# The two ends of a trunk kernel: first weight tile in two transfers, closing root on ScalarE, output in one transfer per column half

## The chip, the cores and the metric

The kernel runs on one core of a Trainium2 chip. The metric is device time in microseconds (us) of one execution, as the median of several runs. Engines are named as the profile names them: PE (TensorE, matmuls) with its weight load PEld, DVE (VectorE), ACT (ScalarE), POOL (GpSimd) and SP (SyncE, which here only issues transfers). Transfers (DMAs) run on 16 DMA engines that the core has.

## The reference

A decoder trunk of two layers on x of 256 tokens by 2048 features, in float32. Each layer adds to x a token mixer (layer 0: chunked gMLP; layer 1: a complex-diagonal S5 state-space layer with a GLU), an attention to 256 memory rows and a squared-ReLU MLP with 8192 hidden features, each on a normalized input. The end is one more normalization. What the change touches of it is the first product and the last line:

```python
def rms_norm(x, g):
    xf = x.astype(F32)
    y = xf * lax.rsqrt(jnp.mean(xf * xf, axis=-1, keepdims=True) + EPS)
    return (y * g.astype(F32)).astype(x.dtype)

def chunked_gmlp(h, w_in, b_in, ln_g, ln_b, w_s, b_s, w_out):
    z = jax.nn.gelu(h @ w_in + b_in, approximate=False)
    u, v = jnp.split(z, 2, axis=-1)
    ...

def reference(x, mem, ...):
    for i in range(DEPTH):
        h = rms_norm(x, g_mix[i])
        x = x + chunked_gmlp(...) if i % 2 == 0 else x + s5_glu(...)
        x = x + memory_attention(...)
        x = x + squared_relu_mlp(rms_norm(x, g_ff[i]), f_w_up[i], f_w_down[i])
    return rms_norm(x, g_final)
```

## The kernel before

**Precision.** A float32 product is made of three float32r products: each operand is split into a high part (a cast on ACT, line 102) and a low part (source less high part, on DVE, line 103), and PE sums high x high, low x high and high x low. So every weight tile goes through three stages: a transfer into `wraw` (line 123), the two splits into `whi` and `wlo`, and the matmuls.

**Tiles.** The weights lie in memory as tiles of 128 partitions by 1024 floats (512 KB): two blocks of 128 input features by 512 output features. `Trunk.wload` issues the transfer of one tile on SP and remembers it as `self.fed`; `Trunk.wtile` loads (or takes a tile that was loaded ahead from the list `raw`) and splits. There are four `wraw` buffers (a fifth in some stages) and three each of `whi` and `wlo`. The order on every engine is the order of the code, moved by a scheduler: it respects the buffers, and `tc.issue_after(self.fed)` puts a transfer behind the weight load named.

**The start.** `gmlp` reads x transposed (`x_t`) in four chunks of four feature blocks; each chunk comes in two transfers of two blocks (128x512, 256 KB; lines 314 to 318, tile `memc`). `scale_chunk` (lines 242 to 249) multiplies each block by the norm's weight and splits it into `act`, on ACT (line 247) and DVE (line 248). Between the two transfers of the first chunk the first weight tile is loaded ahead (`first.append(...)`, line 320). `opening` then works on two column blocks of `a_w_in` in turn, numbers NCH and NCH + 1 (NCH is 4), tile by tile: the first tile of the one, the first of the other, the second of the one, and so on; the matmuls are at line 152. A tile has two feature blocks, so the first tile of either column block needs only the first transfer of x's first chunk.

**The end.** The last matrix product is `gemm_last`: its weights are split once and kept, and it runs over all 16 feature blocks first for token block t = 0 (128 tokens), then for t = 1 (PE lines 829 to 831). After each block it calls `FinalNorm.finish`. There, `gather` (DVE line 658) adds the product to x, 256 columns at a time; ACT squares and sums these (line 1414); DVE adds the two sums to the mean square of the other columns (line 1416), forms an approximate inverse root with an integer trick on the float's bits (line 1417) and refines it in three Newton steps (lines 1421 and 1422, `rstd_t` and `rstd`). x is then multiplied by the root (and, for the last 512 columns, by the norm's weight) in four pieces of 512 columns, two on DVE (lines 1423 and 1425) and two on ACT (lines 1424 and 1427). So block t = 0's closing runs while PE works on t = 1.

**The output.** The tokens lie permuted in x: partition 32q + c of block t is token 8c + 4t + q. A column half of a block is therefore written in four transfers, one for each q: 32 partitions by 1024 columns (128 KB), to every eighth row of the output (line 1430). They are issued on SP:

```python
self.out = out.rearrange("(c h q) d -> h q c d", h=2, q=4)
...
for cs in (slice(0, D // 2), slice(D // 2, D)):
    for q in range(4):
        nc.sync.dma_start(out=self.out[t, q][:, cs], in_=x[32 * q:32 * q + 32, t, cs])
```

**Two other transfers** that the prediction reads are in the S5 layer, the loads of `lb` at line 1054 on SP. Each fills 128 partitions by 512 floats, and its source has a pattern of 8 (T), 16 and 512 elements, the outermost first:

```python
src = (bass.AP(tensor=b.tensor, offset=b.offset, ap=[[0, T], [8 * 64, 16], [1, 8 * 64]]),
       bass.AP(tensor=Ld.tensor, offset=Ld.offset + q * 8 * 64, ap=[[G * 2 * 64, T], [0, 16], [1, 8 * 64]]))
with self.tc.issue_after(self.fed):
    nc.sync.dma_start(out=e["lb", q][:, i], in_=src[i])
```

Of the kernel before, what the change touches and what calls it, by code (L numbers as in the profile page):

```python
# [9 lines left out]
F32 = mybir.dt.float32  # L10
F32R = mybir.dt.float32r
I32 = mybir.dt.int32
AF = mybir.ActivationFunctionType
ALU = mybir.AluOpType
AX = mybir.AxisListType

P = 128
D = 2048
S = 256
KT = D // P  # L20
NB = 512
NCH = D // NB
KB = 2
# [15 lines left out]
class Trunk:  # L39
# [7 lines left out]
    def __init__(self, ctx, tc, a):  # L47
        self.ctx, self.tc, self.nc, self.a = ctx, tc, tc.nc, a
        nc = self.nc
        ent = ctx.enter_context  # L50
        self.const = ent(tc.tile_pool(name="const", bufs=1))
        self.main = ent(tc.tile_pool(name="main", bufs=1))
        self.act = ent(tc.tile_pool(name="act", bufs=2))
        self.wp = ent(tc.tile_pool(name="wp", bufs=3))
        self.sm = ent(tc.tile_pool(name="sm", bufs=2))
        self.dram = ent(tc.tile_pool(name="dram", bufs=1, space=bass.MemoryType.DRAM))
        self.psA = ent(tc.tile_pool(name="psA", bufs=2, space=bass.MemoryType.PSUM))
        self.psM = [ent(tc.tile_pool(name=f"psM{i}", bufs=2, space=bass.MemoryType.PSUM)) for i in range(2)]

        warm = self.const.tile([P, 1], F32, name="warm")  # L60
        nc.vector.memset(warm, 0.0)
        nc.scalar.activation(out=warm, in_=warm, func=AF.Gelu)
        self.ident = self.const.tile([P, P], F32, name="ident")
        make_identity(nc, self.ident)
        self.gcol = self.const.tile([P, 8, KT], F32, name="gcol")
        nc.scalar.dma_start(out=self.gcol, in_=a["gcol"])
        self.rstd_mem = None
        self.loads, self.fifth = 0, None
        self.side = []
        self.lag, self.every, self.now, self.plan = 100, 1, 0, []  # L70
# [42 lines left out]
        return t  # L113


    def wload(self, w, n, kc):
        self.loads += 1
        if self.fifth and self.loads % 5 == 0:
            raw = self.fifth.tile([P, KB * NB], F32, name="wraw", bufs=1)
        else:  # L120
            raw = self.wp.tile([P, KB * NB], F32, name="wraw", bufs=4)
        k, c = w.shape[3:]
        self.fed = self.nc.sync.dma_start(out=raw.rearrange("p (k c) -> p k c", k=k), in_=w[n, kc]).ins
        return raw

    def wtile(self, w, n, kc, raw=None):
        nc = self.nc
        raw = raw.pop() if raw else self.wload(w, n, kc)
        hi = self.wp.tile([P, KB * NB], F32R, name="whi")
        lo = self.wp.tile([P, KB * NB], F32R, name="wlo")  # L130
        self.low = self.split(hi, lo, raw)
        return [t.rearrange("p (k c) -> p k c", k=w.shape[3]) for t in (hi, lo)]

    def gemm_tok(self, act, w, n, acc=None, k0=0, kts=range(KT), first=True, last=True, raw=None):
# [171 lines left out]
    def gmlp(self, x, nxt):  # L306
        nc, a, tc = self.nc, self.a, self.tc
        with tc.tile_pool(name="gm", bufs=2, reuse_waits="tile") as gp:
            hT = self.new_act()
            ss = self.new_ss()  # L310
# [3 lines left out]
            def fetch(j):  # L314
                xt = xts[j] = gp.tile([P, 4, S], F32, name="memc", tag="u", bufs=5)
                for h in range(0, 4, 2):
                    with tc.issue_after(self.fed) if j else nullcontext():
                        nc.sync.dma_start(out=xt[:, h:h + 2], in_=a["x_t"][j][:, h:h + 2])
                    if j == 0 and h == 0:
                        first.append(self.wload(a["a_w_in"], NCH, 0))  # L320

            def features(j):
                self.scale_chunk(xts.pop(j), 0, hT, j)
# [6 lines left out]

            first = []
            fetch(0)
            features(0)
            rstd = None
# [18 lines left out]
            def opening(n0, outs):  # L353

                accs, bs = [None, None], []
                for k in range(NCH):
                    self.at((6, 8, 9, 11)[k], lambda k=k: tokens(k))
                for i in range(2):
                    self.at(10 + i, lambda i=i: bs.append(bias(n0 + i)))

                def step(i, kc):
                    accs[i] = self.gemm_tok(hT, a["a_w_in"], n0 + i, acc=accs[i], kts=range(KB * kc, KB * kc + KB),
                                            first=kc == 0, last=kc == KT // KB - 1, raw=first)

                order = [(i, kc) for kc in range(KT // KB - 2) for i in range(2)]
                order += [(i, KT // KB - 2 + kc) for i in range(2) for kc in range(2)]
                for m, (i, kc) in enumerate(order):
                    if m % 4 == 3 and m // 4 + 1 < NCH:
                        fetch(m // 4 + 1)
                    if m % 4 == 0 and 0 < m < 4 * NCH:  # L370
                        features(m // 4)
                    if m == len(order) - 2:
                        activate(n0, outs[0], accs[0], bs[0])
                    step(i, kc)
                activate(n0 + 1, outs[1], accs[1], bs[1])
# [23 lines left out]
            v = self.act.tile([P, 2, NCH, NB], F32, name="v", tag="act")  # L399
# [973 lines left out]
class FinalNorm:  # L1373
# [4 lines left out]

    def __init__(self, tr, out):
        self.tr = tr  # L1380
        self.out = out.rearrange("(c h q) d -> h q c d", h=2, q=4)

    def start(self):
        tr = self.tr
# [16 lines left out]
    def finish(self, x, t, gather):  # L1401

        tr, nc = self.tr, self.tr.nc
        v = nc.vector
        e = (NCH - 1) * NB
        pre, y, a = (tr.sm.tile([P, 1], F32, name=nm) for nm in ("rs_v", "rstd", "rstd_t1"))
        ss = self.end[:, t]
        v.tensor_reduce(out=pre, in_=self.ss[:, t:t + 1, 0:NCH - 1], axis=AX.X, op=ALU.add)
        v.tensor_scalar(out=pre, in0=pre, scalar1=1.0 / D, scalar2=EPS, op0=ALU.mult, op1=ALU.add)
        for h in range(2):  # L1410
            cs = slice(e + h * NB // 2, e + (h + 1) * NB // 2)
            gather(cs)
            junk = tr.sm.tile([P, NB], F32, name="junk", bufs=1)
            nc.scalar.activation(out=junk[:, 0:NB // 2], in_=x[:, t, cs], func=AF.Square, accum_out=ss[:, h:h + 1])
        for h in range(2):
            v.scalar_tensor_tensor(out=pre, in0=ss[:, h:h + 1], scalar=1.0 / D, in1=pre, op0=ALU.mult, op1=ALU.add)
        v.tensor_scalar(out=y.bitcast(I32), in0=pre.bitcast(I32), scalar1=-0.5,
                        scalar2=1597463007.0, op0=ALU.mult, op1=ALU.add)
        v.tensor_scalar(out=pre, in0=pre, scalar1=-0.5, scalar2=None, op0=ALU.mult)
        for _ in range(3):  # L1420
            v.scalar_tensor_tensor(out=a, in0=y, scalar=pre, in1=y, op0=ALU.mult, op1=ALU.mult)
            v.scalar_tensor_tensor(out=y, in0=a, scalar=1.5, in1=y, op0=ALU.add, op1=ALU.mult)
        v.tensor_scalar(out=x[:, t, 0:NB], in0=x[:, t, 0:NB], scalar1=y, scalar2=None, op0=ALU.mult)
        nc.scalar.activation(out=x[:, t, NB:2 * NB], in_=x[:, t, NB:2 * NB], func=AF.Copy, scale=y)
        v.scalar_tensor_tensor(out=x[:, t, e:], in0=x[:, t, e:], scalar=y, in1=self.g[NCH - 1],
                               op0=ALU.mult, op1=ALU.mult)
        nc.scalar.activation(out=x[:, t, 2 * NB:e], in_=x[:, t, 2 * NB:e], func=AF.Copy, scale=y)
        for cs in (slice(0, D // 2), slice(D // 2, D)):
            for q in range(4):
                nc.sync.dma_start(out=self.out[t, q][:, cs], in_=x[32 * q:32 * q + 32, t, cs])  # L1430


def regroup(tr, x):
# [101 lines left out]
```

## Time and profile before

| | |
|---|---|
| runs | 2793.18, 2794.51, 2795.72 us; median 2794.51 |
| profiled execution | 2790.06 us, of which the span is 2788.4 |
| mean granted clock of PE | 0.999 |
| PE busy | 2765.7 us, 99% of the span |
| DVE, ACT, POOL busy | 71%, 50%, 8% |
| DMA | 593.76 MB, mean 213 GB/s |

The span runs from the first recorded instruction to the end of the last. Busy times are shares of it. Where a row has an "xN", it groups N instructions; the number in front is the time from the first one's start to the last one's end in a timeline, and the sum of their durations in the lists of groups. A DMA share is the mean busy share of the 16 DMA engines in a stretch.

### The profile page before, as it was taken

How to read it: one execution, taken by the hardware profiler on the slowest of the kernel's cores; microseconds unless marked ns; L12 is line 12 of the kernel's file. 1: busy time of each engine (PE TensorE's matmuls, PEld its weight loads, DVE VectorE, ACT ScalarE, POOL GpSimd, SP SyncE). 2: the span in 40 equal slices, each digit the busy share in tenths (PEclk: the TensorE clock that was granted, in tenths of full speed). 3: DMA queues.
4: the chain of work that ended last, by engine and by line, in shares of the span. 5: the costliest groups of instructions: out<-in, count | busy, mean ns of one | idle time of the engine just before them, and what ended most of it. 6: DMA issues, size and time to landing. Idle time of an engine off the chain costs nothing. (4 is left out here: it accounts for less than half of the span.)

```text
span 2788.4 us, 39687 instructions
## 1 busy us (share of the span) xinstructions
PE 2765.7 (99%) x15020; PEld 2331.1 (84%) x15020; DVE 1986.2 (71%) x2747; ACT 1395.3 (50%) x1801; POOL 236.0 (8%) x434
## 2 busy tenths in 40 slices
PE   9999999999999999999999999999999999999998
PEld 7888888888888888888887888888888888888886
DVE  6765756778978878787568657557777767677665
ACT  6545545555534444444555445445555545455454
POOL 0100000001022222231213100000000000000000
PEclk9999999999999999999999999999999999999999
DMA  8766655547688888887879767564556566565655
GB/s 294 226 216 216 204 177 179 177 156 250 212 261 258 258 257 259 259 257 224 244 244 266 218 199 238 173 196 159 177 156 219 168 217 198 166 218 171 218 180 156
DMA packets 196048, 593.76 MB, mean 213 GB/s; under 512 B 44960, under 2 KB 47184, under 8 KB 195344
## 3 DMA queue, kind: packets, MB, share of 16 engines
q1 hardware_dynamic: 151968, 532.22, 60.6%
q0 software_dynamic: 43744, 58.95, 7.7%
q8 instruction: 117, 1.92, 0.3%
q14 instruction: 75, 0.61, 0.1%
q10 hardware_dynamic: 144, 0.07, 0.0%
HBM read 567.51 MB, written 23.46 MB: 212 GB/s over the span
## 5 line engine op out<-in xcount | busy, mean ns | idle before, releaser
L103 DVE TENSOR_TENSOR wlo<-wraw,whi 128x1024 fp32r<-128x1024 f32 x892 | 1085.1, 1222 | 490.0 <-ACT whi L102 484.3
L102 ACT CAST whi<-wraw 128x1024 fp32r<-128x1024 f32 x892 | 936.9, 1052 | 853.5 <-PE acc L723 202.8
L167 PE MATMUL acc<-act,whi 128*128 128x512 f32 x3072 | 742.3, 391 | 0.9 <-ACT whi L102 0.9
L167 PEld LDWEIGHTS acc<-act,whi 128*128 128x128 f32 x3072 | 562.8, 188 | 111.7 <-issue 2.6
L172 PEld LDWEIGHTS acc<-act,wlo 128*128 128x128 f32 x3072 | 394.9, 191 | 17.6 <-DVE wlo L103 1.9
L172 PE MATMUL acc<-act,wlo 128*128 128x256 f32 x3072 | 403.6, 283 | 1.4 <-DVE wlo L103 1.0
L152 PE MATMUL acc<-whi,act 128*128 128x512 f32 x1472 | 369.7, 393 | 7.1 <-ACT whi L102 6.3
L152 PEld LDWEIGHTS acc<-whi,act 128*128 128x128 f32 x1472 | 274.9, 189 | 64.9 <-ACT whi L102 6.3
L723 PE MATMUL acc<-whi,act 128*128 128x512 f32 x864 | 232.9, 392 | 0.0
L807 PE MATMUL acc<-whi,hl 128*128 128x512 f32 x544 | 213.3, 392 | 0.0
L806 PE MATMUL acc<-whi,hh 128*128 128x512 f32 x544 | 212.7, 391 | 0.0
L152 PE MATMUL acc<-wlo,act 128*128 128x512 f32 x736 | 197.1, 389 | 0.0
L723 PEld LDWEIGHTS acc<-whi,act 128*128 128x128 f32 x864 | 160.4, 188 | 36.5 <-ACT ends L755 1.9
L152 PEld LDWEIGHTS acc<-wlo,act 128*128 128x128 f32 x736 | 138.2, 188 | 28.9 <-DVE wlo L103 0.2
L723 PE MATMUL acc<-whi,hh 128*128 128x512 f32 x378 | 148.4, 393 | 0.0
L723 PE MATMUL acc<-whi,hl 128*128 128x512 f32 x378 | 147.2, 390 | 0.0
L809 PE MATMUL acc<-wlo,hh 128*128 128x512 f32 x544 | 145.9, 390 | 0.0
L723 PE MATMUL acc<-wlo,act 128*128 128x512 f32 x432 | 133.1, 390 | 0.0
L807 PEld LDWEIGHTS acc<-whi,hl 128*128 128x128 f32 x544 | 102.1, 188 | 23.0 <-issue 2.2
L183 ACT COPY r<-acc 128x512 f32<-128x512 f32 x64 | 37.7, 588 | 166.6 <-PE acc L167 166.6
L809 PEld LDWEIGHTS acc<-wlo,hh 128*128 128x128 f32 x544 | 102.1, 188 | 21.5 <-issue 0.2
L806 PEld LDWEIGHTS acc<-whi,hh 128*128 128x128 f32 x544 | 102.1, 188 | 21.4 <-issue 0.4
(365 smaller groups left out, 2763.7 us busy)
## 6 DMA issues: line engine op xcount, KB each, us to landing
wraw<-in_f_w_up SPq DMA_DIRECT2D x256, 512.0 KB, 4.6
wraw<-in_f_w_down SPq DMA_DIRECT2D x228, 512.0 KB, 4.6
wraw<-in_a_w_in SPq DMA_DIRECT2D x64, 512.0 KB, 4.7
wraw<-in_x_w_q SPq DMA_DIRECT2D x64, 512.0 KB, 3.9
wraw<-in_x_w_k SPq DMA_DIRECT2D x64, 512.0 KB, 4.6
wraw<-in_b_w_out SPq DMA_DIRECT2D x64, 512.0 KB, 4.4
wraw<-in_x_w_v SPq DMA_DIRECT2D x48, 512.0 KB, 3.9
wraw<-in_x_w_o SPq DMA_DIRECT2D x48, 512.0 KB, 4.3
```

The costliest lines, as they stand in the source:

```text
L102: self.nc.scalar.copy(out=hi, in_=src)
L103: return self.nc.vector.tensor_tensor(out=lo, in0=src, in1=hi.bitcast(F32), op=ALU.subtract).ins
L152: nc.tensor.matmul(out[t], a[:, kt, sl], b[:, kk, :], start=st and a is ah, stop=en)
L167: nc.tensor.matmul(acc[:, f, :], hi[:, kk, sl], both[:, kt].rearrange("p a s -> p (a s)"), start=first and kk == 0, stop=last and kk == FK ...
L172: nc.tensor.matmul(acc[:, f, 0:S], lo[:, kk, sl], ah[:, kt, :], start=False, stop=last and kk == FK - 1, skip_group_check=True)
L183: nc.scalar.copy(out=dst, in_=acc[:, :, S:])
L723: mm = lambda s, m, e: nc.tensor.matmul(out, s, m, start=key not in begun, stop=e, skip_group_check=True)
L806: nc.tensor.matmul(acc[:, t, :], ah, hi[:, kk, :], start=kt == 0, stop=False)
L807: nc.tensor.matmul(acc[:, t, :], al, hi[:, kk, :], start=False, stop=False)
L809: nc.tensor.matmul(acc[:, t, :], hid[kt // 4][0][:, kt % 4, sl], lo[:, kk, :], start=False, stop=kt == KT - 1)
```

## The change

Three pieces of code are changed.

1. *The first weight tile.* `wload` can split its transfer into `pieces`; the first tile is loaded in two transfers of one feature block each (128x512, 256 KB), and `wtile` casts and subtracts it in two halves. The first tile of the second column block (NCH + 1) is now loaded ahead as well, right behind the first, and so before x's second pair of feature blocks.
2. *The closing root.* The sum of the first half's squares goes into `pre` as before. ACT then takes the square root of the whole mean (`AF.Sqrt`, with the second half's sum as its input and `pre` as its bias); DVE forms the same mean beside it, takes the reciprocal of ACT's root and makes one Newton step.
3. *The output.* A column half of a block leaves in one transfer of 128 partitions by 1024 columns. The access pattern of the output in it is 4 (q), 32 (c) and 1024, the outermost first.

```diff
-    def wload(self, w, n, kc):
+    def wload(self, w, n, kc, pieces=1):
...
         k, c = w.shape[3:]
-        self.fed = self.nc.sync.dma_start(out=raw.rearrange("p (k c) -> p k c", k=k), in_=w[n, kc]).ins
+        dst = raw.rearrange("p (k c) -> p k c", k=k)
+        for i in range(0, k, k // pieces):
+            r = slice(i, i + k // pieces)
+            self.fed = self.nc.sync.dma_start(out=dst[:, r], in_=w[n, kc][:, r]).ins
         return raw
 
     def wtile(self, w, n, kc, raw=None):
         nc = self.nc
+        opening = len(raw) == 2 if raw else False
         raw = raw.pop() if raw else self.wload(w, n, kc)
...
-        self.low = self.split(hi, lo, raw)
+        n = KB * NB // KB if opening else KB * NB
+        for i in range(0, KB * NB, n):
+            self.low = self.split(hi[:, i:i + n], lo[:, i:i + n], raw[:, i:i + n])
...
                     if j == 0 and h == 0:
-                        first.append(self.wload(a["a_w_in"], NCH, 0))
+                        first.append(self.wload(a["a_w_in"], NCH, 0, pieces=KB))
+                        first.insert(0, self.wload(a["a_w_in"], NCH + 1, 0))
...
-        self.out = out.rearrange("(c h q) d -> h q c d", h=2, q=4)
+        self.out = out
+
+    def rows(self, t, cs):
+
+        o = self.out
+        return bass.AP(tensor=o.tensor, offset=o.offset + 4 * t * D + cs.start,
+                       ap=[[D, 4], [8 * D, 32], [1, cs.stop - cs.start]])
...
+        root = tr.sm.tile([P, 1], F32, name="root", bufs=1)
...
-        for h in range(2):
-            v.scalar_tensor_tensor(out=pre, in0=ss[:, h:h + 1], scalar=1.0 / D, in1=pre, op0=ALU.mult, op1=ALU.add)
-        v.tensor_scalar(out=y.bitcast(I32), in0=pre.bitcast(I32), scalar1=-0.5,
-                        scalar2=1597463007.0, op0=ALU.mult, op1=ALU.add)
-        v.tensor_scalar(out=pre, in0=pre, scalar1=-0.5, scalar2=None, op0=ALU.mult)
-        for _ in range(3):
-            v.scalar_tensor_tensor(out=a, in0=y, scalar=pre, in1=y, op0=ALU.mult, op1=ALU.mult)
-            v.scalar_tensor_tensor(out=y, in0=a, scalar=1.5, in1=y, op0=ALU.add, op1=ALU.mult)
+        v.scalar_tensor_tensor(out=pre, in0=ss[:, 0:1], scalar=1.0 / D, in1=pre, op0=ALU.mult, op1=ALU.add)
+        nc.scalar.activation(out=root, in_=ss[:, 1:2], func=AF.Sqrt, scale=1.0 / D, bias=pre)
+        v.scalar_tensor_tensor(out=a, in0=ss[:, 1:2], scalar=1.0 / D, in1=pre, op0=ALU.mult, op1=ALU.add)
+        v.tensor_scalar(out=pre, in0=a, scalar1=-0.5, scalar2=None, op0=ALU.mult)
+        v.reciprocal(out=y, in_=root)
+        v.scalar_tensor_tensor(out=a, in0=y, scalar=pre, in1=y, op0=ALU.mult, op1=ALU.mult)
+        v.scalar_tensor_tensor(out=y, in0=a, scalar=1.5, in1=y, op0=ALU.add, op1=ALU.mult)
...
         for cs in (slice(0, D // 2), slice(D // 2, D)):
-            for q in range(4):
-                nc.sync.dma_start(out=self.out[t, q][:, cs], in_=x[32 * q:32 * q + 32, t, cs])
+            nc.sync.dma_start(out=self.rows(t, cs), in_=x[:, t, cs])
```

How it moves instructions shows at three places. SP at the start, before (`memc` is x's transposed chunk, `wraw` a weight tile; a row with xN stands for N in a row):

```order
L318 DMA memc<-in_x_t 128x512
L123 DMA wraw<-in_a_w_in 128x1024
L318 DMA memc<-in_x_t 128x512
L123 DMA wraw<-in_a_w_in 128x1024 x2
L318 DMA memc<-in_x_t 128x512 x2
L123 DMA wraw<-in_a_w_in 128x1024 x3
```

SP at the start, after the change:

```order
L324 DMA memc<-in_x_t 128x512
L126 DMA wraw<-in_a_w_in 128x512 x2
L126 DMA wraw<-in_a_w_in 128x1024
L324 DMA memc<-in_x_t 128x512
L126 DMA wraw<-in_a_w_in 128x1024
L324 DMA memc<-in_x_t 128x512 x2
L126 DMA wraw<-in_a_w_in 128x1024 x3
```

The first tile is two rows, and x's second piece has moved behind the second tile; the third tile's place is the same.

DVE on the closing of token block 1, before (`ss` the sums of squares, `rs_v` the mean square, `rstd` the inverse root):

```order
L1416 SCALAR_TENSOR_TENSOR rs_v<-ss,rs_v 128x1 x2
L1417 TENSOR_SCALAR rstd<-rs_v 128x1
L1419 TENSOR_SCALAR rs_v<-rs_v 128x1
L1421 SCALAR_TENSOR_TENSOR rstd_t_24691<-rstd,rs_v 128x1
L1422 SCALAR_TENSOR_TENSOR rstd<-rstd_t_24691,rstd 128x1
L1421 SCALAR_TENSOR_TENSOR rstd_t_24691<-rstd,rs_v 128x1
L1422 SCALAR_TENSOR_TENSOR rstd<-rstd_t_24691,rstd 128x1
L1421 SCALAR_TENSOR_TENSOR rstd_t_24691<-rstd,rs_v 128x1
L1422 SCALAR_TENSOR_TENSOR rstd<-rstd_t_24691,rstd 128x1
```

and after the change, where `root` is ACT's result:

```order
L1429 SCALAR_TENSOR_TENSOR rs_v<-ss,rs_v 128x1
L1431 SCALAR_TENSOR_TENSOR rstd_t_24686<-ss,rs_v 128x1
L1432 TENSOR_SCALAR rs_v<-rstd_t_24686 128x1
L1433 RECIPROCAL rstd<-root 128x1
L1434 SCALAR_TENSOR_TENSOR rstd_t_24686<-rstd,rs_v 128x1
L1435 SCALAR_TENSOR_TENSOR rstd<-rstd_t_24686,rstd 128x1
```

Ten steps have become six, and the reciprocal waits for ACT. ACT's whole end, both token blocks, after the change:

```order
L1428 ACTIVATE junk,ss<-x 128x256 x2
L1430 ACT_TABLE_LOAD
L1430 ACTIVATE root<-ss,rs_v 128x1
L1437 ACTIVATE x<-x,rstd 128x512
L1440 ACTIVATE x<-x,rstd 128x512
L1428 ACTIVATE junk,ss<-x 128x256 x2
L1430 ACTIVATE root<-ss,rs_v 128x1
L1437 ACTIVATE x<-x,rstd 128x512
L1440 ACTIVATE x<-x,rstd 128x512
```

The roots stand between the squares and the scalings, and one load of an activation table is ahead of the first. On SP the program's last rows were `L1430 DMA out<-x 32x1024 x16` and are now `L1442 DMA out<-x 4x32x1024 x4`. Nothing else in the program changes its order.

## The prediction

> **What bounds the kernel now.** I read the page's busy times first, then the table of stretches, the waits of PE, the timeline of the first 11 us and of the last 20, and the DMA share there. The page:
>
> ```profile
> span 2788.4 us, 39687 instructions
> PE 2765.7 (99%) x15020; PEld 2331.1 (84%) x15020; DVE 1986.2 (71%) x2747; ACT 1395.3 (50%) x1801; POOL 236.0 (8%) x434
> ```
>
> PE is idle for 2788.4 - 2765.7 = 22.7 us in all. The table of stretches (start:end, length, then busy us of PE, PEld, DVE, ACT, POOL, the granted clock, DMA share, GB/s) and PE's waits say where:
>
> ```profile
> 0.00:10.00 10.00, 3.65 (x9) 2.89 (x10) 3.06 (x6) 5.09 (x8) 1.40 (x7) 1.00 0.79 289
> 2766.00:2777.30 11.30, 11.28 (x50) 9.01 (x48) 3.79 (x14) 2.36 (x6) 0.00 (x0) 1.00 0.34 93
> 2777.30:2788.40 11.10, 0.00 (x0) 0.00 (x0) 3.78 (x14) 2.35 (x6) 0.00 (x0) 0.69 0.35 95
> PE acc L152 <- ACT whi L102: 6.3, 1, 6.3
> PE ps L152 <- ACT whi L102: 1.2, 1, 1.2
> ```
>
> 6.3 us before PE's first matmul, 11.1 us after its last one, and about 5 us in small waits between, the longest 1.2 us. The change touches neither the middle nor PE's instructions, so it can only move the 6.3 us ahead of PE and the 11.1 us behind it. In the tail PE is gone, and DMA moves 95 GB/s at a third of its engines' time: two things take turns there, a chain on DVE and ACT, then a transfer out.
>
> **The head.** Timeline (start, length, engine, line; in brackets idle time and releaser):
>
> ```profile
> 0.82 0.41 SPq L318 DMA_DIRECT2D memc<-in_x_t  x1
> 1.28 0.42 SPq L123 DMA_DIRECT2D wraw<-in_a_w_in  x1
> 3.74 0.91 ACT L247 ACTIVATE act<-memc,gcol 128x256 fp32r<-128x256 f32 x2 [1.00 <-DMA memc<-in_x_t]
> 5.25 1.04 ACT L102 CAST whi<-wraw 128x1024 fp32r<-128x1024 f32 x1 [0.60 <-DMA wraw<-in_a_w_in]
> 6.35 3.75 PE L152 MATMUL acc<-whi,act 128*128 128x512 f32 x8 [6.35 <-ACT whi L102]
> 9.26 1.05 ACT L102 CAST whi<-wraw 128x1024 fp32r<-128x1024 f32 x1 [0.40 <-DMA wraw<-in_a_w_in]
> 10.87 2.00 PE L152 MATMUL acc<-whi,act 128*128 128x512 f32 x8
> L102 ACT CAST hh<-r 128x512 fp32r<-128x512 f32 x64 | 39.5, 617 | 10.6 <-DVE r L641 10.6
> ```
>
> ACT scales x's first pieces from 3.74 to 4.65, idles 0.60 us for the 512 KB weight tile and casts it in 1.04; then PE starts. The last row is a cast of 512 columns elsewhere: 0.62 us. With the tile in two transfers the first half is there earlier: if it lands by 4.65, the cast runs 4.65 to 5.27 and PE starts at about 5.28, 1.05 us sooner. If it lands late, the gain shrinks towards the 0.42 us by which the cast itself is shorter. The second half's cast (to 5.89) is well ahead of PE, which takes 3.75 us over its first eight matmuls. One DMA more goes through SP, 0.42 us, ahead of everything that follows. The second tile now is ahead of x's second pieces: before, it landed at 9.26, after 1.5 MB, and PE wanted it cast at 10.87 (cast over at 10.31). PE will want it at 9.8; with 256 KB less ahead of it, at the 317 GB/s of the second ten microseconds
>
> ```profile
> 10.00:20.00 10.00, 10.00 (x46) 8.24 (x45) 7.61 (x9) 8.37 (x14) 0.00 (x0) 1.00 0.92 317
> ```
>
> it lands 0.8 us sooner, at about 8.5, and is cast by 9.55: hidden by 0.25 us. If that cover is missing, the wait of PE takes the gain back, so the head's bounds are 0 and -1.1 us. I take **-1.05**, because both covers hold by the rows.
>
> **The closing root.** Tail, second token block, on DVE and ACT:
>
> ```profile
> 2778.76 0.19 ACT L1414 ACTIVATION_READ_ACCUMULATOR junk<-x 128x1 f32 x1
> 2778.97 0.16 DVE L1416 SCALAR_TENSOR_TENSOR rs_v<-ss,rs_v 128x1 f32<-128x1 f32 x1 [0.38 <-ACT junk L1414]
> 2780.44 0.22 DVE L1421 SCALAR_TENSOR_TENSOR rstd_t<-rstd,rs_v 128x1 f32<-128x1 f32 x1
> 2780.70 0.16 DVE L1422 SCALAR_TENSOR_TENSOR rstd<-rstd_t,rstd 128x1 f32<-128x1 f32 x1
> 2780.89 0.72 ACT L1424 ACTIVATE x<-x,rstd 128x512 f32<-128x512 f32 x1 [1.95 <-DVE rstd L1422]
> L523 ACT ACT_TABLE_LOAD x2 | 2.6, 1283 | 0.0
> L62 ACT ACTIVATE warm<-warm 128x1 f32<-128x1 f32 x1 | 0.2, 203 | 0.0
> L526 DVE RECIPROCAL rsm<-smx 128x2 f32<-128x2 f32 x8 | 1.3, 167 | 8.1 <-ACT e L523 8.1
> ```
>
> From the last square's sum (2778.95) to the first scaling of x (2780.89) are 1.94 us: nine short DVE steps in a row, each 0.15 to 0.22 with some 0.04 between. After: the root on ACT (0.20, as the 128x1 activation), with the two DVE steps that do not need it beside it; then reciprocal (0.17), one L1421 (0.22), one L1422 (0.16) and four gaps: about 1.0 us. So the second block's x is scaled about 0.95 us sooner, first output issue at 2780.7 in place of 2781.64. In the first block a table load (1.28 us) stands ahead of the root, on ACT between the squares and the root: 1.28 + 1.0 against 1.94 makes that block's x some 0.3 us later. Behind it on ACT are only that block's own scalings, and PE runs past them on the second block, so it costs PE nothing. What is late is the first block's first output issue: 2771.1 for 2770.77.
>
> **The output.** All of it, both blocks, in a window over the tail, and its first issue:
>
> ```profile
> 2770.77 14.46 SPq L1430 DMA_DIRECT2D out<-x  x16
> GB/s 0 0 0 0 0 0 0 241 177 265 305 257 265 281 257 8 0 0 0 0 0 0 0 0 0 0 0 0 177 209 233 265 249 321 233 321 48 16 0 0
> DMA packets 769, 2.11 MB, mean 103 GB/s; under 512 B 256, under 2 KB 256, under 8 KB 768
> q1 hardware_dynamic: 768, 2.10, 38.0%
> ```
>
> The window is 2768 to 2788.4, a slice 0.51 us. Each block leaves in eight slices, about 4.3 us. Data start 1.1 us after the first issue, and the span ends 1.3 us after the last data. The 256 packets under 512 B are the closing packets: 16 to each of 16 transfers, so each of today's transfers is spread on all 16 DMA engines. The busy time is 0.380 x 16 x 20.4 = 124 engine-us for 2.10 MB, 16.9 GB/s for an engine at work.
>
> The new transfer has 4 as the outermost count of its access pattern in the output, then 32 rows, then columns. The trace holds one kind of transfer with a small outermost count, the two `lb` loads, whose source has 8 outermost, ahead of 16 and a row. Window 740.5 to 755.6:
>
> ```profile
> DMA packets 1127, 3.65 MB, mean 241 GB/s; under 512 B 112, under 2 KB 112, under 8 KB 1126
> q1 hardware_dynamic: 1126, 3.63, 81.0%
> wraw<-in_f_w_down SPq DMA_DIRECT2D x5, 512.0 KB, 5.9
> lb<-in_b_pc SPq DMA_DIRECT2D x1, 256.0 KB
> lb<-Ld SPq DMA_DIRECT2D x1, 256.0 KB
> ```
>
> 3.63 MB is six weight tiles of 0.524 MB (one issued just before the window) and two lb loads of 0.262. Six tiles with 16 closing packets make 96; the 16 left of the 112 are the two lb loads', 8 each. So a transfer whose outermost count is 8 ran on 8 engines, not 16. By that row a transfer with 4 outermost runs on 4.
>
> [...]
>
> On four engines, both blocks go through the same four, since the first block's 1.05 MB is not out when the second's is issued, 9.6 us later. So the end is no longer the second block's chain: it is the first block's first issue, the time X of 2.10 MB on four engines, and the close. The price of X by rows:
>
> - at the rate of all engines in the best slices of the weight stream, below (about 426 GB/s, 26.6 for one of 16 engines): 2.10 MB / (4 x 26.6 GB/s) = 19.7 us;
> - at the output's own mean, 124 engine-us / 4 = 31.0 us;
> - at the rate of today's first output transfers, alone in 0.7 us: 0.941 x 16 x 0.7 = 10.5 engine-us for 0.14 MB, 13.3 GB/s; X = 39.5 us.
>
> ```profile
> GB/s 397 397 459 344 41 180 164 344 397 336 381 307 336 344 324 291 246 274 352 426 426 397 406 434 397 426 410 393 401 414 410 365 418 385 348 344 295 369 385 397
> q1 hardware_dynamic: 51, 0.14, 94.1%
> ```
>
> (The first row is the window 10 to 30 us, the second 2782.7 to 2783.4.) I take 31.0: it is the same data in the same direction, some packets alone and some beside others, and lies between the ends.
>
> Sum: 2771.1 + 1.1 + 31.0 + 1.3 = 2804.5, less 1.05 for the head = 2803.45, against the span of 2788.4: **+15.1 us**. The saving of SP's issues (twelve fewer of some 0.42 us) and the 0.95 us of the second block's root lie inside the 31 us and count nothing.
>
> **Basis.** The profiled execution took 2790.06 us, the runs 2793.18 to 2795.72, median 2794.51. The difference is put on the median: 2794.5 + 15.1 = **2809.6 us**, 0.54% slower. What can be told from no change is about 0.2%, 5.6 us.
>
> **The rivals.**
>
> - A, four engines at the full rate. For it: the weight stream's slices. Against: the output's own mean is lower. X = 19.7: 2794.5 + 3.8 = 2798.3. Slower, yet within 0.2%.
> - B, four engines that get in each other's way. For it: the 13.3 GB/s of the first transfers, when 16 engines work on only 32 partitions. Against: the mean over both blocks is better. X = 39.5: 2794.5 + 23.6 = 2818.1. [...]
> - C, the transfers are spread on 16 engines after all, or each on another four. Then the change does what its parts say: head -1.05, second block's root -0.95, and two issues in place of eight ahead of the last transfer. The last of eight at 0.42 is issued 2.9 us behind the first, the last of two 0.4; data of a block would take 1.05 MB / 426 GB/s = 2.5 us for 4.3, a gain of up to 1.8. Together -2.0 to -3.8, 2794.5 - 3 = 2791.5. For it: twelve fewer descriptors of work for SP and every output row in today's trace on 16. Against: the 8 closing packets of the lb loads. It decides the case if the closing packets are 64 (16 to each of four) or the data of both blocks are out in 5 us each.
>
> **How the numbers follow.** Forecast 0.42, A 0.22, B 0.24, C 0.10, anything else 0.02. The likeliest one's own range is 2803 to 2815. The range, 2797 to 2820, reaches to A and B, which the unknown rate of an engine on this work spans, and leaves out C. Faster by over 0.2%: 0.04 (the far end of C and a lucky remainder). Within 0.2%: 0.24 (most of A and of C). Slower: 0.72.
>
> **What would show it.** In the profile after: 16 closing packets under 512 B (4 to each of 4) in place of 256 and about a quarter of the DMA share through the whole tail, up to the span's end, without the gap of 6.5 us between the blocks; the second block's first issue about 0.95 us sooner after its PE end; a table load once, in the first block; PE's first matmul at about 5.3 us and no new wait for the second weight tile. Wrong would be the forecast if the output shows over half of the engines busy, or a rate per engine outside 13 to 27 GB/s; the head, if PE starts later than 5.9 or waits for its second tile at about 10 us.

## The result, and the profile after

The changed kernel takes 2819.31 us (median, 2818.52 to 2820.60) beside 2794.61 us for the kernel before: +24.7 us, a ratio of 1.0091 with a 95% interval of 1.0076 to 1.0106. It is slower, as forecast, but by more than the 15.1 us forecast, and most of the loss is at a place of which the prediction said that nothing could happen there. Times and ratios here and below are of the fast runs; two runs of the experiments, of 8707 and 3035 us, fell in a slow state and are left out.

The page of the changed kernel, and its table of stretches (columns as in the prediction):

```profile
span 2817.5 us, 39676 instructions
PE 2785.7 (99%) x15020; PEld 2332.3 (83%) x15020; DVE 1986.2 (70%) x2740; ACT 1396.1 (50%) x1805; POOL 234.3 (8%) x434
```

```profile
2777.30:2797.75 20.45, 20.45 (x88) 16.16 (x86) 7.79 (x20) 6.61 (x14) 0.00 (x0) 1.00 0.07 16
2797.75:2817.50 19.75, 0.02 (x1) 0.00 (x0) 2.95 (x10) 2.65 (x7) 0.00 (x0) 0.56 0.22 92
```

The span grew by 2817.5 - 2788.4 = 29.1 us (the profiled execution of before was some 4 us under its median). PE now ends at 2797.8 in place of 2777.3: **20.5 us of it are PE's**. The stretch behind PE is 19.7 us in place of 11.1: **8.6 us are the tail's**. PE has the same 15020 matmuls and as little idle time; it was busy 20.0 us longer, at a granted clock of 1.00.

Which matmuls? Groups of PE, before first, then after (busy us, then mean ns of one; names are accumulator<-moving operand,weights held):

```profile
L807 PE MATMUL acc<-whi,hl 128*128 128x512 f32 x544 | 213.3, 392 | 0.0
L806 PE MATMUL acc<-whi,hh 128*128 128x512 f32 x544 | 212.7, 391 | 0.0
L809 PE MATMUL acc<-wlo,hh 128*128 128x512 f32 x544 | 145.9, 390 | 0.0
L723 PE MATMUL acc<-whi,hh 128*128 128x512 f32 x378 | 148.4, 393 | 0.0
L723 PE MATMUL acc<-whi,hl 128*128 128x512 f32 x378 | 147.2, 390 | 0.0
L723 PE MATMUL acc<-wlo,hh 128*128 128x512 f32 x378 | 116.4, 389 | 0.0
```

```profile
L814 PE MATMUL acc<-whi,hl 128*128 128x512 f32 x544 | 216.6, 398 | 0.0
L813 PE MATMUL acc<-whi,hh 128*128 128x512 f32 x544 | 216.0, 397 | 0.0
L816 PE MATMUL acc<-wlo,hh 128*128 128x512 f32 x544 | 149.3, 396 | 0.0
L730 PE MATMUL acc<-whi,hh 128*128 128x512 f32 x378 | 150.0, 397 | 0.0
L730 PE MATMUL acc<-whi,hl 128*128 128x512 f32 x378 | 149.6, 396 | 0.0
L730 PE MATMUL acc<-wlo,hh 128*128 128x512 f32 x378 | 118.8, 396 | 0.0
L730 PE MATMUL acc<-whi,act 128*128 128x512 f32 x864 | 232.8, 392 | 0.0
```

All matmuls of the MLPs that hold `hh` or `hl` (the two parts of the hidden features) as weights are slower by 4 to 7 ns each; the six rows add up to 16.4 us. Of the other 3.6 us, 0.9 are in the last product (three rows of 32 with hh or hl, 396 ns for 389), and the rest is a few tenths each in other rows. The row with `act` in place of `hh`, from the same source line, did not change (232.9 us before). Layer 0's rows with hh and hl lie at 752 to 1390 us, layer 1's from 2171 us on, and none of these instructions was changed. What was changed is where their tiles lie. `root`, a new tile of 4 bytes a partition, takes a slot of 32 bytes in the pool of small tiles, and every pool behind it starts 32 bytes later. Start addresses in bytes in the two programs, with the remainder by 512 (`hh` and `hl` of layer 1; layer 0's first `hh` moves alike, from 188352 to 188384, remainders 448 and 480):

```
tile    before           after
act     37312   (448)    37312   (448)
whi     119232  (448)    119232  (448)
wlo     131520  (448)    131520  (448)
root    -                146240
hh      146368  (448)    146400  (480)
hl      162752  (448)    162784  (480)
```

The tail (issues on SP; then DMA in the window 2792 to 2817.5, a slice is 0.64 us):

```profile
2791.34 11.04 SPq L1442 DMA_DIRECT2D out<-x  x4
GB/s 19 51 39 77 58 26 58 51 64 84 96 103 109 109 103 103 109 103 109 103 103 103 109 109 103 103 109 103 109 103 103 103 109 109 84 51 58 45 0 0
DMA packets 528, 2.10 MB, mean 82 GB/s; under 512 B 16, under 2 KB 16, under 8 KB 528
q1 hardware_dynamic: 528, 2.10, 22.4%
```

16 closing packets in place of 256, four for each of four transfers, and no gap between the blocks: the output runs on four engines (a DMA share of 0.25 to 0.26 of the 16 from 2797.75 to 2814 us), one block right behind the other. From first to last data are 23.6 us (2792.6 to 2816.2), of which some 15 in the middle at 103 to 109 GB/s, 26 for an engine. The first 6 us are slower, at 19 to 84 GB/s, and so are the last 2.5, at 84 down to 45. Packet by packet, a row of 4 KB takes 0.30 us in the mean of the first 5 us (67 rows) and 0.16 from PE's last matmul (2797.8) on, which comes 5.2 us behind the first packet. In the two other profiles with four transfers the rate goes up 5 to 6 us behind the first data too: with the output alone from 17 to 68 GB/s, up to 2778.7 us, to mostly 90 to 113; in the change without its 32 bytes from 23 to 75, up to 2784.3 us, to mostly 103 to 109. Whether PE's end or the time since the first packet matters, these profiles do not tell.

The head (start, length, engine, line):

```profile
4.50 0.91 ACT L253 ACTIVATE act<-memc,gcol 128x256 fp32r<-128x256 f32 x2 [1.74 <-DMA gcol<-in_gcol]
5.96 3.78 PE L158 MATMUL acc<-whi,act 128*128 128x512 f32 x8 [5.96 <-ACT whi L102]
9.54 1.87 PE L158 MATMUL acc<-wlo,act 128*128 128x512 f32 x4
11.25 2.01 PE L158 MATMUL acc<-whi,act 128*128 128x512 f32 x8
```

PE began 0.39 us sooner and reached its second tile 0.38 us later than before (10.87), though that tile's cast was over at 8.82. The first twelve matmuls are all some 0.43 us apart, where before the pace went to 0.23 after eight.

### The profile page after: what moved, and what is told of

Read it like the earlier page. It is cut to its first block, busy times and chain, and to the rows that moved or that the text cites. A ratio compares the mean times of both kernels' runs of the same rounds, so it can differ in the third digit from the quotient of the medians.

```text
span 2817.5 us, 39676 instructions
## 1 busy us (share of the span) xinstructions
PE 2785.7 (99%) x15020; PEld 2332.3 (83%) x15020; DVE 1986.2 (70%) x2740; ACT 1396.1 (50%) x1805; POOL 234.3 (8%) x434
## 5 line engine op out<-in xcount | busy, mean ns | idle before, releaser
L103 DVE TENSOR_TENSOR wlo<-wraw,whi 128x1024 fp32r<-128x1024 f32 (+1 forms) x893 | 1086.1, 1221 | 502.1 <-ACT whi L102 497.8
L102 ACT CAST whi<-wraw 128x1024 fp32r<-128x1024 f32 (+1 forms) x893 | 936.6, 1051 | 872.8 <-PE acc L730 210.1
L158 PE MATMUL acc<-whi,act 128*128 128x512 f32 x1472 | 369.7, 393 | 6.7 <-ACT whi L102 6.0
L814 PE MATMUL acc<-whi,hl 128*128 128x512 f32 x544 | 216.6, 398 | 0.0
L730 PE MATMUL acc<-whi,hl 128*128 128x512 f32 x378 | 149.6, 396 | 0.0
L813 PEld LDWEIGHTS acc<-whi,hh 128*128 128x128 f32 x544 | 102.1, 188 | 24.7 <-issue 0.4
```

Source lines behind the costliest of these rows:

```text
L102: self.nc.scalar.copy(out=hi, in_=src)
L103: return self.nc.vector.tensor_tensor(out=lo, in0=src, in1=hi.bitcast(F32), op=ALU.subtract).ins
L158: nc.tensor.matmul(out[t], a[:, kt, sl], b[:, kk, :], start=st and a is ah, stop=en)
L730: mm = lambda s, m, e: nc.tensor.matmul(out, s, m, start=key not in begun, stop=e, skip_group_check=True)
L813: nc.tensor.matmul(acc[:, t, :], ah, hi[:, kk, :], start=kt == 0, stop=False)
L814: nc.tensor.matmul(acc[:, t, :], al, hi[:, kk, :], start=False, stop=False)
```

## The experiments

Theory **address**: the new tile's 32 bytes move hh and hl, and that makes PE slow; the output on four engines makes the tail long; head and root are worth about nothing. Rival **change**: the slow matmuls come from the head, the root or the output. The kernel before ran beside each set, at medians of 2792.5 to 2793.8 us, given with each.

### The spare tile alone

```diff
         pre, y, a = (tr.sm.tile([P, 1], F32, name=nm) for nm in ("rs_v", "rstd", "rstd_t1"))
+        root = tr.sm.tile([P, 1], F32, name="root", bufs=1)
+        v.memset(root, 0.0)
```

> The kernel before, plus one unused tile of 4 bytes a partition in the pool of the small tiles (set to zero once per token block on DVE), where the change has its root tile. All tiles placed behind that pool, hh and hl among them, start 32 bytes later. Theory 'address' (the matmuls that take hh or hl as weights slow from 0.227 to 0.233 us because these tiles now start at an odd multiple of 32 bytes): about +17 to +20 us, 2812 to 2815 us, PE's last matmul 17 to 20 us later, the tail behind PE still 11.1 us. Rival 'change' (the slower matmuls come from the head, the root or the output itself): as before, 2793 to 2796. Rival 'clock' (a slower granted clock): as before, or slower matmuls on every line alike.

2811.68 us beside 2792.48: ratio 1.0068 (1.0053 to 1.0083), +19.2 us. Nothing of the change is in this kernel but 32 bytes (and the instruction that sets the tile to zero), and its rows are those of the changed kernel:

```profile
PE 2785.9 (99%) x15020; PEld 2332.3 (83%) x15020; DVE 1987.8 (71%) x2749; ACT 1396.4 (50%) x1801; POOL 236.4 (8%) x434
L807 PE MATMUL acc<-whi,hl 128*128 128x512 f32 x544 | 216.6, 398 | 0.0
L723 PE MATMUL acc<-whi,act 128*128 128x512 f32 x864 | 232.9, 392 | 0.0
```

### The whole change, but no tile moves

```diff
-        root = tr.sm.tile([P, 1], F32, name="root", bufs=1)
         ss = self.end[:, t]
+        root = ss[:, 2:3]
...
-        self.end = tr.sm.tile([P, 2, 2], F32, name="ss")
+        self.end = tr.sm.tile([P, 2, 3], F32, name="ss")
```

(against the changed kernel; `end` had room for the third column in its slot.)

> The whole change, but the root is kept in a spare column of a tile that is there already (end), so that no tile moves. Theory 'address': the tail's share of the loss alone, 8.6 us (19.7 us behind PE's last matmul for 11.1) and 0.4 us of the head: 2803 to 2804. Rival 'change': 2818 to 2821, as the change is. What the four-engine forecast itself said for the output, X = 31 us, would give 2810.

2802.34 us beside 2792.48, ratio 1.0033 (1.0019 to 1.0047): +9.9 us where 9 were expected, and 14.8 us less of a loss than the changed kernel's 24.7. The MLP's rows are back at 389 to 393 ns. The change without its 32 bytes is still slower, by the output.

### Head and root, the output as before

```diff
         for cs in (slice(0, D // 2), slice(D // 2, D)):
-            nc.sync.dma_start(out=self.rows(t, cs), in_=x[:, t, cs])
+            for q in range(4):
+                nc.sync.dma_start(out=self.out[t, q][:, cs], in_=x[32 * q:32 * q + 32, t, cs])
```

(against the kernel of the experiment above.)

> The change's head and root (in the spare column), with the sixteen output transfers of before. Theory 'address': head +0.4, second block's root -0.9: within 1 us of before, 2793 to 2796. Rival 'change', with head or root as the cause of the slower matmuls: 2811 to 2815.

2790.16 us beside 2792.48, ratio 0.9991 (0.9981 to 1.0001): 2.3 us faster by the medians, not told apart from no change, nor from the -2.0 that the prediction has for head and root together.

### The output alone

```diff
-            for q in range(4):
-                nc.sync.dma_start(out=self.out[t, q][:, cs], in_=x[32 * q:32 * q + 32, t, cs])
+            nc.sync.dma_start(out=self.rows(t, cs), in_=x[:, t, cs])
```

> The kernel before with only the output changed: four transfers with 4 outermost. No tile moves. Theory 'four engines': the first block's issue at 2770.8, 1.1 us to the first data, 23.7 us for 2.10 MB as in the change's profile, 1.3 us to the end: 2796.9 for a span of 2788.4, +8.5 us, 2803 us; 16 packets under 512 B in the tail. By my recorded X of 31 us: 2810. If the output also were the cause of the slower matmuls: 2815 or more.

2801.42 us beside 2792.48, ratio 1.0036 (1.0023 to 1.0049): +8.9 us. Its SP issue, and DMA from 2770 to its end at 2799.1:

```profile
2772.32 12.06 SPq L1435 DMA_DIRECT2D out<-x  x4
DMA packets 528, 2.10 MB, mean 72 GB/s; under 512 B 16, under 2 KB 16, under 8 KB 528
q1 hardware_dynamic: 528, 2.10, 20.1%
```

The first packet starts at 2773.6 us and the last one ends at 2797.8: 24.2 us for the data. An engine's own time is 0.201 x 16 x 29.1 = 93.6 engine-us, 23.4 us each on four.

### The head alone

The changes to `wload`, `wtile` and `fetch` as in the diff above, nothing else.

> The change's head alone. My recorded term was -1.05 us. In the change's profile PE began 0.4 us sooner, but its slow first matmuls (0.43 us apart) lasted to 11.24 us instead of 10.17, so PE was 0.4 us behind by its thirteenth: between -0.4 and +0.4 us, 2792 to 2793.5 beside a before of 2792.5. That would show PE's full pace to come at a time of its own, whatever its first matmul. -1.05 or better would show the change's own profile to be a bad draw.

2792.35 us beside 2792.66, ratio 0.9995 (0.9987 to 1.0004): no difference that can be told; the interval, -3.6 to +1.1 us, holds both zero and the -1.05 of the prediction. In its profile the scaling did not wait for `gcol`, and PE began when the prediction said:

```profile
5.32 3.78 PE L158 MATMUL acc<-whi,act 128*128 128x512 f32 x8 [5.32 <-ACT whi L102]
8.89 1.52 PE L158 MATMUL acc<-wlo,act 128*128 128x512 f32 x4
10.25 1.98 PE L158 MATMUL acc<-whi,act 128*128 128x512 f32 x8
```

The start is 1.03 us sooner (6.35 before), the second tile 0.62 (10.87 before). One profile of each kernel does not price the head, but all the kernels of this case together say more, ten with the old head and five with the new:

| | old head | mean | new head | mean |
|---|---|---|---|---|
| ACT's first scaling starts (us) | 3.62 to 4.14 | 3.76 | 3.79 to 4.64 | 4.31 |
| PE's first matmul | 6.30 to 6.74 | 6.43 | 5.32 to 6.11 | 5.79 |
| first matmul of the second tile | 10.70 to 11.79 | 11.22 | 10.25 to 11.25 | 10.65 |

So the new head is worth about 0.6 us in the mean, at the start and at the second tile alike. The forecast start of 5.28 was met in one profile of five; in the others ACT's first scaling began later for x's first piece or for `gcol` (in the changed kernel at 4.50, with 1.74 us of waiting). The spread at the second tile is mostly PE's pace. With either head it goes from 0.43 to 0.23 us a matmul after 7 to 14 matmuls, 3.1 to 6.1 us behind the first; why it goes up when it does, no run shows. The granted clock in the prediction's table of stretches is 1.00 over the first 10 us and does not show it; the spacing of the matmuls does. The changed kernel's profile, with twelve slow matmuls for eight before, hid its gain by chance.

### The root alone

The root in `end`'s spare column as above, head and output as before.

> The root on ACT alone, kept in the spare column, sixteen output transfers. Second block's first output issue 0.95 us sooner behind PE's last matmul, so -0.9 us; with the head's e3 gave a ratio of 0.9991 (-2.3 us). If the root alone gives about that, the head gives nothing; if it gives 0.9, the head gives the rest.

2791.26 us beside 2792.66, ratio 0.9997 (0.9989 to 1.0006): no difference that can be told; the expected -0.9 us lies in the interval. With this root the second block takes 1.06 us from the last square's sum to the first scaling (2799.38 to 2800.44 in the changed kernel's profile), for 1.94 before.

### The second column half issued on ACT

```diff
-        for cs in (slice(0, D // 2), slice(D // 2, D)):
+        for cs, queue in ((slice(0, D // 2), nc.sync), (slice(D // 2, D), nc.scalar)):
             for q in range(4):
-                nc.sync.dma_start(out=self.out[t, q][:, cs], in_=x[32 * q:32 * q + 32, t, cs])
+                queue.dma_start(out=self.out[t, q][:, cs], in_=x[32 * q:32 * q + 32, t, cs])
```

(against head and root with the old output.)

> Head and root as in the change (root in the spare column), sixteen transfers, those of the second column half issued on ACT's queue in place of SP's. The last of a block's eight is then issued some 1 us sooner (four behind four, at 0.42 us each, less ACT's later start): the last data about 1 us sooner, -3 us against before. If transfers and not issues set the pace of the 4.3 us: as with one queue, -2.3.

2790.12 us beside 2792.66, ratio 0.9992 (0.9983 to 1.0001). Beside the 0.9991 of one queue no gain shows; what remains of head and root together is at the edge of what can be told.

### hh alone, 32 bytes lower

```diff
-            r2 = mp.tile([P, 32 if layer else 56], F32, name="r2", bufs=1)[:, 0:2]
+            r2 = mp.tile([P, 24 if layer else 48], F32, name="r2", bufs=1)[:, 0:2]
...
                     h = mp.tile([P, 4, S], F32R, name="hh")
+                    if not n + b:
+                        pad = mp.tile([P, 8], F32, name="pad", bufs=1)
```

> The kernel before, where only the four hh tiles of the MLPs start 32 bytes lower (a tile ahead of them is cut by 32 bytes, a pad of 32 follows), and hl, sums, own and all else stay. If an odd start of the weights' own tile slows the matmul: rows with hh about 397 ns for 391 and rows with hl unchanged; hh is two of three matmuls of these products (544 and 378 of each row, some 1900 in all), so about two thirds of the spare tile's 19 us, 11 to 14 us: 2804 to 2807. If instead the distance between hh and hl, or all tiles together, matter: hl rows slow too, or neither.

2808.89 us beside 2792.66, ratio 1.0057 (1.0042 to 1.0073): +16.2 us, more than two thirds of 19.2. The rows with hl, which did not move, are as slow as those with hh:

```profile
L809 PE MATMUL acc<-whi,hl 128*128 128x512 f32 x544 | 216.9, 399 | 0.0
L808 PE MATMUL acc<-whi,hh 128*128 128x512 f32 x544 | 215.2, 396 | 0.0
L725 PE MATMUL acc<-whi,act 128*128 128x512 f32 x864 | 232.9, 392 | 0.0
```

hh and hl take turns as weights (line 807 behind line 806), so a matmul with hl runs while PE loads hh for the next (in the kernel before, a matmul of line 807 starts at 752.63 us and takes 0.39, and the load of hh for line 806 starts at 752.63 and takes 0.19). A row does not say which of two neighbours is at fault. My theory had the cost in the rows of the moved tile, and that part fell.

### hh alone, 64 bytes lower

As above, with 16 and 40 floats for `r2` and a pad of 16 floats.

> As the run with hh 32 bytes lower, but 64 bytes lower (a pad of 64 follows), so that hh starts again at a multiple of 64. Theory 'odd multiple of 32': no slowing, hh and hl rows at 390 to 393 ns, as before, 2791 to 2795. Theory 'another place' (any move of hh against hl or against the other tiles costs): as with 32 bytes, +16 us, 2808.

2802.35 us beside 2793.78, ratio 1.0033 (1.0020 to 1.0045): +8.6 us. Neither of the two: not nothing, as "odd multiple of 32" had it, and half of what 32 bytes cost.

```profile
L809 PE MATMUL acc<-whi,hl 128*128 128x512 f32 x544 | 214.4, 394 | 0.0
L808 PE MATMUL acc<-whi,hh 128*128 128x512 f32 x544 | 214.8, 395 | 0.0
```

### hl alone, 32 bytes higher

```diff
                     h = mp.tile([P, 4, S], F32R, name="hh")
+                    if not n + b:
+                        pad = mp.tile([P, 8], F32, name="pad", bufs=1)
```

> The kernel before with a pad of 32 bytes between hh and hl: hh stays, hl and the tiles behind it (sums, own, r) start at an odd multiple of 32. hh is the weights of two matmuls of three, hl of one. With hh alone moved, +16.2 us, and with both +19.2: if the costs of the two add up, +3 us, 2795 to 2797; if each by itself disturbs the alternation of hh and hl, +8 to +16, 2800 to 2809.

2808.21 us beside 2793.78, ratio 1.0058 (1.0038 to 1.0078): +14.4 us. hl is the weights of one matmul in three and costs nearly what hh does; the two do not add up. Even the rows with wlo and hh, which neither stream nor hold a moved tile, are slower (before: 145.9 us, 390 ns and 116.4 us, 389 ns):

```profile
L808 PE MATMUL acc<-whi,hh 128*128 128x512 f32 x544 | 216.0, 397 | 0.0
L811 PE MATMUL acc<-wlo,hh 128*128 128x512 f32 x544 | 147.1, 392 | 0.0
L725 PE MATMUL acc<-wlo,hh 128*128 128x512 f32 x378 | 117.9, 393 | 0.0
```

So the loss is not confined to the matmuls whose own two operands changed their distance.

### whi and wlo, 32 bytes higher

```diff
+        if self.loads == 1:
+            pad = self.wp.tile([P, 8], F32, name="pad", bufs=1)
         hi = self.wp.tile([P, KB * NB], F32R, name="whi")
...
-            r2 = mp.tile([P, 32 if layer else 56], F32, name="r2", bufs=1)[:, 0:2]
+            r2 = mp.tile([P, 24 if layer else 48], F32, name="r2", bufs=1)[:, 0:2]
```

> The kernel before with a pad of 32 bytes ahead of whi and wlo (the tiles behind them in other pools move too; hh and hl are put back to their places). whi and wlo are the weights held by PE on lines 167 and 172 (3072 matmuls each) and the moving operand on lines 152, 723, 806 to 809. Theory 'weights': only line 167 slows, by 6 ns of 227, and line 172 if it has no slack, 18 to 37 us: 2811 to 2830, and lines 152 and 806 to 809 stay. Theory 'either operand': those slow too, 30 us more. If the rule is one of hh and hl alone: as before.

2836.68 us beside 2793.78, ratio 1.0161 (1.0142 to 1.0181): +42.9 us. It slows whi as the weights held and as the moving operand alike (before: 742.3, 369.7, 232.9 and 212.7 us):

```profile
L169 PE MATMUL acc<-act,whi 128*128 128x512 f32 x3072 | 756.1, 396 | 0.6 <-ACT whi L102 0.6
L154 PE MATMUL acc<-whi,act 128*128 128x512 f32 x1472 | 378.3, 398 | 7.1 <-ACT whi L102 6.3 <-ACT u L1184 0.8
L725 PE MATMUL acc<-whi,act 128*128 128x512 f32 x864 | 237.1, 396 | 0.0
L808 PE MATMUL acc<-whi,hh 128*128 128x512 f32 x544 | 216.0, 397 | 0.0
```

In the first three rows act stayed, in the last hh did. So it is not a matter of the weights alone; two readings are left: either operand at an odd start slows the matmul, or what counts is how the two lie to each other.

### Every tile 32 bytes higher

```diff
         warm = self.const.tile([P, 1], F32, name="warm")
+        pad = self.const.tile([P, 8], F32, name="pad")
```

> The kernel before with a spare tile of 32 bytes at the very start of the on-chip memory, so that every tile of the kernel, act, whi, wlo, hh and hl alike, starts 32 bytes later. Theory 'odd start' (a matmul slows when one of its two operands starts at an odd multiple of 32): every one of the 128x512 rows slows, as 18 to 43 us with whi and wlo moved, and hh, hl and act on top of it: 2830 to 2860 us. Theory 'relative place' (the slowing depends on how the weights held and the moving operand lie to each other; before the change all of them have the same remainder by 512, and moving hh by -64 cost half of what -32 did): nothing moves relative to anything, so as before, 2791 to 2796, all rows at 389 to 393 ns.

2793.04 us beside 2793.75, ratio 1.0000 (0.9990 to 1.0009). All five tiles start at an odd multiple of 32 bytes now, and no row is slow:

```profile
L168 PE MATMUL acc<-act,whi 128*128 128x512 f32 x3072 | 742.4, 392 | 0.3 <-ACT whi L103 0.3
L808 PE MATMUL acc<-whi,hl 128*128 128x512 f32 x544 | 213.3, 392 | 0.0
L807 PE MATMUL acc<-whi,hh 128*128 128x512 f32 x544 | 212.7, 391 | 0.0
```

This decides it: hh starts at the very address here (146400) at which it was slow in the changed kernel. The place of a tile by itself costs nothing that can be told; **what costs is how the tiles that PE reads lie to each other**. Which pair of them counts (the moving operand against the weights held, or against the next weights, loaded meanwhile) the runs do not separate.

### hh 128 bytes lower in layer 0, 96 in layer 1

As with 32 bytes, with 8 and 24 floats for `r2` and pads of 24 and 32 floats (layer 1 and layer 0).

> The kernel before with hh moved against all else by -128 bytes in layer 0 (rows of lines 806 to 809 with 512 matmuls in the layer) and by -96 in layer 1 (line 723 with hh, 378 each). Theory 'relative place, remainder by 128': layer 0 as before (391, 392, 390 ns), layer 1 as with 32 bytes (395 to 397). Theory 'remainder by 64': layer 0 as before, layer 1 as with 32 bytes, but then -64 should have cost nothing, and it cost 9 us. Theory 'any difference costs, by its size': layer 0 slow too, 394 ns or more. In the time: 16 us x the share of layer 1 (6.3 us of it): about +6 under the first, +12 or more under the last.

2805.96 us beside 2793.30, ratio 1.0044 (1.0027 to 1.0062): +12.7 us.

```profile
L809 PE MATMUL acc<-whi,hl 128*128 128x512 f32 x544 | 216.4, 398 | 0.0
L808 PE MATMUL acc<-whi,hh 128*128 128x512 f32 x544 | 215.4, 396 | 0.0
L725 PE MATMUL acc<-whi,hl 128*128 128x512 f32 x378 | 149.0, 394 | 0.0
```

128 bytes (layer 0, the first two rows; 512 of their 544 matmuls are in that layer) cost nearly as much as 32. So an equal remainder by 128 is not enough. In the kernel before, all five tiles have an equal remainder by 512 while hh and whi differ by 27136 bytes, 53 x 512, so that a difference of that multiple of 512 has none of this loss. What 256 would cost was not tried.

## Why the prediction was right or wrong, point by point

**"The change touches neither the middle nor PE's instructions, so it can only move the 6.3 us ahead of PE and the 11.1 us behind it."** This step failed, and with it most of the 24.7 us: a term that I had at nothing. PE's instructions are the same, but their operands' addresses are not: the spare tile alone gives +19.2 us, and the change without the shift of addresses +9.9. I compared the two programs by the order of their instructions, in which names and shapes stand but no address. The code had a hint that I did not read: `r2` is 56 or 32 floats wide and two of them are used; the rest is what put hh at the same remainder as whi.

**The count of engines: right.** Eight for the lb loads pointed to four for the output; the 16 closing packets and the missing gap show it, and the output alone costs +8.9 us. The sum put both blocks through the same four engines, for which no row of before was evidence; the changed kernel's profile shows it: the second block's last issue is at 2801.8 us, the eighth of the 16 closing packets comes at 2806.3, and the DMA share of the 16 engines is 0.25 ahead of that issue and 0.26 in both blocks' data behind it.

**X, 31.0 us: too large.** 23.6 us in the changed kernel, 24.2 with the output alone. I divided the 124 engine-us of sixteen engines by four, as if a packet took as long on four engines as on sixteen. It took 0.24 us in the mean on sixteen engines, and 0.16 on four for most of the time. That is 26 GB/s each, the upper end of my bounds (26.6), so rival A was nearer: it had 19.7 us at that rate throughout, without the slow start and the slow last stretch. What makes the start slow is not settled. With X as measured, my sum would have been 7.4 us lower, some 2802, which is where the runs with the output alone (2801.4) and with the change without its shift (2802.3) lie. That the total still came out near my upper bound is luck: one term of 19 us that I had at nothing, and one that was 7.4 us too large.

**Rival B: wrong, though the time fits it.** It gave 2818.1 and 2819.3 were measured, by two other causes. Four engines at some 13 GB/s each are there in the first 5 us (0.30 us for 4 KB), but not beyond, where it is 26: a time that fits is no evidence for a mechanism, the rate in the tail is.

**Rival C** is out by the closing packets.

**The head, -1.05: right in kind, too large.** PE's first matmul came at 5.32 us in the run of the head alone (5.28 forecast), but at 5.61 to 6.11 in the four other profiles with this head. The step that fell short is ACT's first scaling at 3.74: it began at 4.31 in the mean of the five, since x's first piece or `gcol`, a transfer that I had not counted, landed later; why, no run shows. In the mean the head brings about 0.6 us. The +0.4 of the changed kernel's profile is one draw of PE's slow first matmuls, which I had read in the row of 3.75 us for eight and used only to cover the second half's cast. By the time the head cannot be told from nothing (0.9995).

**The root: right, and hidden as said.** 1.06 us for 1.94, a gain of 0.88 (0.95 forecast); the root activation took 0.29 us in place of the 0.20 assumed. In the first block 2.34 us for 1.95 (+0.39 for +0.3), with a table load of 1.28 us in it. Neither can be seen behind the four engines' queue, and the root alone gives 0.9997, which does not tell -0.9 us from nothing.

In sum, by the profiles: PE's slow matmuls +20.1, head +0.4, tail +8.6, together 29.1, against -1.05 and +16.1 forecast for the last two. By the runs the spare tile (+19.2) and the output (+8.9) add up to 28.1; the 24.7 of the whole change has an interval of 21 to 30 us, which holds both sums.

## What to carry to other kernels

A change that adds a tile, however small, can move the tiles that are placed behind it (here 4 bytes a partition moved them by 32): compare the start addresses of the matmuls' operands before and after, not the order of instructions alone, and look at the mean of one matmul by row, where 391 to 397 ns in rows that nobody touched is 20 us. Look at the number that stands outermost in a transfer's access pattern: here 32 ran on sixteen engines, 8 on eight and 4 on four, and four large transfers on four engines were worse than sixteen small ones on sixteen. And a gain of a microsecond at the start is not read from one profile: the first matmul of the second tile lay between 10.70 and 11.79 us with one and the same head, mostly by PE's slow first matmuls.

## What was not expected of the hardware

A matmul of 128x512 in float32r starts 0.227 us behind the one before it (the median of its row) in the kernel before, where act, whi, wlo, hh and hl start at an equal remainder by 512 bytes; with every tile moved by 32 bytes the rows with hh and hl take 389 to 393 ns, as before. In the changed kernel the matmuls with hh and hl are 0.232 to 0.235 us apart. Where a part of these tiles is moved by 32, 96 or 128 bytes against the others, the rows of the MLPs with a moved tile take 394 to 400 ns, and 392 to 396 at 64 (+8.6 us where 32 bytes give +16.2). The kernel before has two small groups that lie off: `msums` and the `sums` of the attention to memory, at remainder 384, 64 bytes from whi; their matmuls with whi are 0.231 us apart in the median, and 0.234 in the changed kernel, where 32 bytes are left. For the 128x256 matmuls with wlo held (line 172) a difference of 32 bytes cost nothing: 400.2 us for 403.6 with whi and wlo moved. Why it is so, and why matmuls slow whose own two tiles did not move, these runs do not tell.
